# The mixers' channel-major projections and half of the gates, taken first as pairs of blocks by Strassen's seven products and passed on through DRAM

## The chip, the core and the metric

The kernel runs on one core of a Trainium2 chip. The metric is the device time of one execution in microseconds (us). Before the change the median of three runs is 2567.64 us (2566.79 to 2568.14). The engines are PE (TensorE, matmuls), DVE (VectorE), ACT (ScalarE), POOL (GpSimd) and SP (SyncE, which here only issues DMAs).

## What is computed

One layer of a streaming encoder on x of 1024 tokens by 1024 channels, float32. Cut to what matters:

```python
h = rmsnorm(x)
(hg_q, hg_f, hg_i, hg_g, ml_qk, ml_v, ml_if, ml_o,
 mb_z, mb_xbc, mb_dt, gate_pre) = split(h @ w_in)       # w_in: 1024 x 13336
o_hg = hgrn2_scan(silu(hg_q), log_f(hg_f), hg_i)         # 8 heads
y_hg = rmsnorm(o_hg) * silu(hg_g)
qk   = silu(causal_dwconv(ml_qk))                        # conv of width 4 over the tokens
y_ml = rmsnorm(mlstm_scan(qk, ml_v, ml_if)) * sigmoid(ml_o)                     # 4 heads
xbc  = silu(causal_dwconv(mb_xbc))                       # conv of width 4
y_mb = rmsnorm((ssd_scan(xbc, mb_dt) + d * xs) * silu(mb_z))                    # 4 groups
gates = sigmoid(gate_pre)                                # 3 x 1024 channels
mixed = gates[0]*(y_hg @ w_br_hg) + gates[1]*(y_ml @ w_br_ml) + gates[2]*(y_mb @ w_br_mb)
x = x + mixed @ w_out
x = x + (silu(u_g) * u_v) @ w_down                       # u = causal_dwconv(rmsnorm(x) @ w_up)
return rmsnorm(x)
```

## The kernel before

Channels lie on the 128 partitions, tokens along the free dimension. A weight block is 128x1024: all 1024 inputs (eight k tiles of 128) for 128 output channels. Every operand of a large product is split into two parts (`split`, L98 to L100): `hi` is a copy by ACT in the type fp32r, `lo` the rest, by DVE; a product is then hi·hi + hi·lo + lo·hi, three matmuls. `gemm` (L136) multiplies one block with all tokens: 8 k tiles x 3 x 2 halves of 512 tokens = 48 matmuls of 128x512 into `ps_g`, two banks of PSUM (`pg`, two such buffers). `gemm_tok` (L168) makes values with tokens on partitions, from pairs of blocks `w_v`. `weight` (L104 to L112) loads a block on SP's queue into `w_raw` (pool `wr`, three buffers) and splits it into `w_hi`, `w_lo` (pool `ws`, two).

The stages follow one another. `first` loads and normalizes x, splits it into h (four tiles of 128x8x512) and makes the first head's blocks f and q and its values. Then come 8 HGRN2 heads (`hg_head`), 4 mLSTM heads (`ml_head`) and 4 Mamba-2 groups (`mb_group`); after them the branches, each with its gate (`gate`, one block each, 24 in all), w_out, and the MLP. Each mixer makes its own blocks: an HGRN2 head three (f, q, g), an mLSTM head four (two with a conv of width 4, whose later taps are `scalar_tensor_tensor` operations at L502), a Mamba group four, all with a conv: 24 + 16 + 16 = 56 blocks. So the blocks and the `w_v` products of the next head stand in PE's queue between the small matmuls of this one, and fill the time in which a mixer's own chain runs on DVE and ACT. Of an HGRN2 head these small matmuls are the transposes of `kd` (L325), six levels with `pa` (L361, L370), the output (L380, L382), and, behind its norm, the transposes of `out_ch` (L604), which go on to DRAM as `y_dram` by a DMA on POOL's queue. Of a Mamba group they are, among others, L664, L677 and L693.

What sets the order: the mixers are written one after another, and a scheduler with its own timeline reorders the instructions of each engine by their readiness; `high_priority` lets the loading and splitting of weights come 200 places earlier. Each engine then runs its queue strictly in order. `mp` are the mixers' buffers (BUFS: one to four of a name).

## Time and profile before

| | |
|---|---|
| median of three runs | 2567.64 us |
| the profiled execution | 2567.49 us, of which the span is 2565.7 us |
| busy: PE, PE's weight loads, DVE, ACT, POOL | 2537.4, 2177.3, 1282.1, 882.1, 21.8 us |
| mean DMA rate | 64 GB/s |

The span is the profiler's stretch from the first to the last recorded work; 1.8 us lie around it. A busy time is the sum of an engine's instructions, and engines overlap. The chain that ended last is followed back from the last instruction, at each step to what released it. "Lnnn" is a line of the kernel; the lines of before and of the changed kernel are numbered apart.

### The profile page before, as it was taken

The numbers are of one execution on the slowest core, as the hardware profiler recorded it, in microseconds if no ns is written. First come the engines' busy times: TensorE is split into PE (matmuls) and PEld (weight loads), VectorE is DVE, ScalarE is ACT, GpSimd is POOL, SyncE is SP. The second block draws the span as 40 slices with busy tenths as digits, with TensorE's granted clock in tenths as the row PEclk, the third lists the DMA queues.
The fourth block names the chain that finished last, engine by engine and source line by source line (L and its number), as shares of the span: only waits on it lengthen the run. The fifth ranks groups of instructions, "written<-read, shape, count | busy, mean of one in ns | idle before, by whom it ended". The sixth has DMA issues, their size and how long they took to land.

```text
span 2565.7 us, 30851 instructions
## 1 busy us (share of the span) xinstructions
PE 2537.4 (99%) x13304; PEld 2177.3 (85%) x13304; DVE 1282.1 (50%) x1586; ACT 882.1 (34%) x1055; POOL 21.8 (1%) x35
## 2 busy tenths in 40 slices
PE   8999999999999999999999999999999999999998
PEld 7898989898889899899888888888788888888886
DVE  6676767773334466666412223235644444434446
ACT  5444444553343346445312112123332212121212
POOL 1000000000000000000000000000000000000000
PEclk8999999999999999999999999999999999999998
DMA  3011111111121122212412213132211111111111
GB/s 140 33 42 42 42 42 42 52 50 65 59 74 67 41 90 83 83 50 74 132 50 80 80 46 115 50 107 99 66 50 50 50 44 48 49 50 50 50 50 66
DMA packets 47592, 163.59 MB, mean 64 GB/s; under 512 B 5448, under 2 KB 6088, under 8 KB 47456
## 3 DMA queue, kind: packets, MB, share of 16 engines
q1 hardware_dynamic: 44000, 149.04, 17.2%
q0 software_dynamic: 3456, 12.58, 1.3%
q8 instruction: 104, 1.70, 0.3%
q14 instruction: 32, 0.26, 0.0%
HBM read 144.72 MB, written 16.88 MB: 63 GB/s over the span
## 4 chain that ended last, share of the span: by engine, by line
PE 97%; DVE 2%; ACT 1%; issue 0%; DMA 0%; DVEq 0%; SPq 0%; ACTq 0%
PE ps_g L136 70%; PE ps_g L168 9%; PE ps_m L136 5%; PE ps_m L361 3%; PE ps_m L693 1%; PE ps_m L168 1%; PE ps_m L370 1%; PE ps_m L604 1%; PE ps_m L575 1%; PE ps_m L380 1%; PE ps_m L333 0%; PE ps_m L555 0%; PE ps_m L577 0%; PE ps_m L677 0%; PE ps_m L664 0%; PE ps_m L382 0%
## 5 line engine op out<-in xcount | busy, mean ns | idle before, releaser
L136 PE MATMUL ps_g<-h,w_hi 128*128 128x512 f32 x2592 | 722.0, 396 | 3.5 <-DVE h L100 2.0
L99 ACT CAST w_hi<-w_raw 128x1024 fp32r<-128x1024 f32 x209 | 218.5, 1046 | 1049.0 <-PE ps_g L136 938.5
L136 PEld LDWEIGHTS ps_g<-h,w_hi 128*128 128x128 f32 x2592 | 484.4, 188 | 103.4 <-ACT h L99 3.1
L100 DVE TENSOR_TENSOR w_lo<-w_raw,w_hi 128x1024 fp32r<-128x1024 f32 x209 | 255.3, 1222 | 536.6 <-ACT w_hi L99 536.3
L136 PE MATMUL ps_g<-h,w_lo 128*128 128x512 f32 x1296 | 411.0, 394 | 0.0
L136 PE MATMUL ps_g<-p_hi,w_hi 128*128 128x512 f32 x1088 | 338.2, 390 | 0.7 <-DVE u L502 0.5
L136 PE MATMUL ps_g<-p_lo,w_hi 128*128 128x512 f32 x1088 | 337.6, 389 | 0.8 <-DVE p_lo L100 0.8
L136 PE MATMUL ps_g<-p_hi,w_lo 128*128 128x512 f32 x1088 | 337.8, 389 | 0.0
L136 PEld LDWEIGHTS ps_g<-h,w_lo 128*128 128x128 f32 x1296 | 243.7, 188 | 50.4
L168 PE MATMUL ps_g<-w_hi,h 128*128 128x256 f32 x1408 | 261.1, 284 | 0.0
L136 PEld LDWEIGHTS ps_g<-p_hi,w_hi 128*128 128x128 f32 x1088 | 204.1, 188 | 44.1 <-ACT w_hi L99 0.9
L136 PEld LDWEIGHTS ps_g<-p_lo,w_hi 128*128 128x128 f32 x1088 | 204.2, 188 | 43.6 <-DVE p_lo L100 1.1
L136 PEld LDWEIGHTS ps_g<-p_hi,w_lo 128*128 128x128 f32 x1088 | 204.1, 188 | 42.6 <-DVE w_lo L100 0.3
L168 PEld LDWEIGHTS ps_g<-w_hi,h 128*128 128x128 f32 x1408 | 221.3, 192 | 0.6
L168 PE MATMUL ps_g<-w_lo,h 128*128 128x256 f32 x704 | 200.1, 284 | 0.0
L168 PEld LDWEIGHTS ps_g<-w_lo,h 128*128 128x128 f32 x704 | 134.9, 192 | 0.5
L502 DVE SCALAR_TENSOR_TENSOR u<-ps_g,c_vec,u 128x1023 f32<-128x1023 f32 (+2 forms) x90 | 113.0, 1255 | 5.2 <-ACT u L498 3.7
L857 DVE TENSOR_TENSOR x<-ps_g,x 128x1024 f32<-128x1024 f32 x40 | 48.9, 1223 | 99.9 <-PE ps_g L136 99.9
L136 PE MATMUL ps_g<-a_hi,w_hi 128*128 128x512 f32 x288 | 88.8, 389 | 1.6 <-DVE x L857 1.6
L136 PE MATMUL ps_g<-a_lo,w_hi 128*128 128x512 f32 x288 | 88.7, 389 | 0.0
L136 PE MATMUL ps_g<-a_hi,w_lo 128*128 128x512 f32 x288 | 88.7, 389 | 0.0
L756 DVE TENSOR_TENSOR gate<-ps_g,gate 128x1024 f32<-128x1024 f32 x16 | 19.6, 1225 | 128.0 <-PE ps_g L136 128.0
(279 smaller groups left out, 2838.9 us busy)
## 6 DMA issues: line engine op xcount, KB each, us to landing
w_raw<-w_up SPq DMA_DIRECT2D x44, 512.0 KB, 3.4
w_raw<-w_hg SPq DMA_DIRECT2D x24, 512.0 KB, 3.4
w_raw<-w_v SPq DMA_DIRECT2D x24, 512.0 KB, 3.5
ta<-rows SPq DMA_DIRECT2D x24, 512.0 KB, 4.6
w_raw<-w_gate SPq DMA_DIRECT2D x24, 512.0 KB, 3.5
w_raw<-w_br SPq DMA_DIRECT2D x24, 512.0 KB, 3.5
w_raw<-y_dram SPq DMA_DIRECT2D x24, 512.0 KB, 3.5
w_raw<-w_down SPq DMA_DIRECT2D x22, 512.0 KB, 3.4
```

The lines of the kernel that those rows point to most:

```text
L99: self.nc.scalar.copy(out=hi, in_=src)
L100: (eng or self.nc.vector).tensor_tensor(out=lo, in0=src, in1=hi.bitcast(F32), op=ALU.subtract)
L136: self.nc.tensor.matmul(out=out, lhsT=w[:, ks], rhs=rhs(part, kt, ts), start=kt == 0 and w is hi and part == 0, stop=kt == kts - 1 and w i ...
L168: self.nc.tensor.matmul(out=out, lhsT=self.h[hf][part][:, 4 * i + k, o:o + P], rhs=w[:, ks], start=start and k == 0 and w is hi and part = ...
L361: nc.tensor.matmul(out=pa[0:m, c], lhsT=z[:, c * P:c * P + m], rhs=part(1)[:, c], start=True, stop=True)
L370: nc.tensor.matmul(out=pa[:, j], lhsT=c3(k)[:, c + j], rhs=qs[:, c + j], start=True, stop=True)
L380: nc.tensor.matmul(out=po[:, j], lhsT=A[:, c], rhs=v[:, c, vs], start=True, stop=c == 0)
L502: nc.vector.scalar_tensor_tensor(out=out[:, a:ts.stop], in0=ps[:, a - d:ts.stop - d], scalar=w(d), in1=out[:, a:ts.stop], op0=ALU.mult, op ...
L575: nc.tensor.matmul(out=po, lhsT=A[:, c], rhs=v[:, c], start=True, stop=c == 0)
L604: nc.tensor.transpose(out=pt[:, j], in_=src(4 * hf + j), identity=self.ident)
L693: nc.tensor.matmul(out=pa[:, c], lhsT=A[:, c], rhs=xd[:, c, hl * 64:hl * 64 + 64], start=True, stop=True)
L857: nc.vector.tensor_tensor(out=x2[j], in0=ps, in1=x2[j], op=ALU.add)
```

## The change

A pair of neighbouring blocks, 256 output channels, is now multiplied with all tokens by Strassen's scheme (in Winograd's form). The pair is cut in four parts by k half and block, h in four by k half and token half. Seven products of 4 k tiles x 3 matmuls of 128x512, with sums and differences of parts, replace the eight that two blocks take (96 matmuls become 84). The differences of h (t1 to t4, split into hi and lo) are made once, in `first`. For each pair, `operands` splits one block as it is (`w`), one half of the other (`q`), and makes four half-block sums on DVE, which are split as `s` and `r`; `w` has two buffers, `q`, `s` and `r` one. `pair_gemm` issues the seven products, with three half-block copies by ACT and four half-block sums by DVE between them, and a last copy by ACT.

`projections` runs between `first` and the mixers. It takes 33 pairs: 11 of HGRN2 (its first two blocks are still made in `first`), 4 of mLSTM's output gates, 6 of the branch gates (blocks 12 to 23), and 12 with a conv (4 of mLSTM, 8 of Mamba). The activations and convs are done there, and each result goes to DRAM by a DMA on POOL's queue (`keep`). The mixers fetch them on SP's queue (`fetch`). Values of the first two pairs of HGRN2 heads go through DRAM too. The other 12 gates are made by `gemm` between the HGRN2 heads (`GATES_AT`); all 24 are fetched in the branches. The mixers' buffers are allocated only after the pairs, since the t tiles (`tp`) and the pairs' buffers (`a1`) lie in their place.

Where the order moves. On PE, at the start of the projections, behind the norm of the second half of h: before, `h_84` to `h_87` are h's four tiles, and the matmuls alternate between halves.

```order
L136 MATMUL ps_g<-h_84,w_hi 128x512 x2
L136 MATMUL ps_g<-h_85,w_hi 128x512
L136 MATMUL ps_g<-h_84,w_lo 128x512
L136 MATMUL ps_g<-h_84,w_hi 128x512
L136 MATMUL ps_g<-h_85,w_hi 128x512
L136 MATMUL ps_g<-h_84,w_lo 128x512
```

After, the same place holds the value products of the second pair of HGRN2 heads, and the pairs follow; the first mixer stands behind them all:

```order
L172 MATMUL ps_g<-h,w_hi 128x512 x2
L172 MATMUL ps_g<-h,w_lo 128x512
L172 MATMUL ps_g<-h,w_hi 128x512 x2
L172 MATMUL ps_g<-h,w_lo 128x512
L172 MATMUL ps_g<-h,w_hi 128x512 x2
L172 MATMUL ps_g<-h,w_lo 128x512
```

So no block product of `gemm` is left beside the pairs. On DVE, in the middle of `projections`, where a conv pair meets the next pair's operands (`gate` is a pair's result, L161 makes the sums, L102 the lo parts, L636 is the conv's taps, `u` a partial result):

```order
L102 TENSOR_TENSOR q_lo<-w_raw,q_hi 128x512
L161 TENSOR_TENSOR w_raw<-w_raw 128x512 x2
L185 TENSOR_TENSOR gate<-ps_g,u 128x512
L636 SCALAR_TENSOR_TENSOR gate<-c,c_vec,gate 128x1023
L102 TENSOR_TENSOR s_lo<-w_raw,s_hi 128x1024
L636 SCALAR_TENSOR_TENSOR gate<-c,c_vec,gate 128x1022
L102 TENSOR_TENSOR r_lo<-w_raw,r_hi 128x1024
L636 SCALAR_TENSOR_TENSOR gate<-c,c_vec,gate 128x1021
L102 TENSOR_TENSOR w_lo<-w_raw,w_hi 128x1024
L161 TENSOR_TENSOR w_raw<-w_raw 128x512
L185 TENSOR_TENSOR u<-ps_m,u 128x512
L161 TENSOR_TENSOR w_raw<-w_raw 128x512
```

The conv's taps, which before stood beside a mixer's own work (L502), here stand between the lo parts of the next pair's s, r and w. On PE, at the end of the fourth HGRN2 head, before: the output's last matmuls, then block products, then the transposes of the norm (L604):

```order
L136 MATMUL ps_g<-h_84,w_hi 128x512
L136 MATMUL ps_g<-h_86,w_hi 128x512
L136 MATMUL ps_g<-h_85,w_hi 128x512
L136 MATMUL ps_g<-h_87,w_hi 128x512
L136 MATMUL ps_g<-h_84,w_lo 128x512
L136 MATMUL ps_g<-h_86,w_lo 128x512
L136 MATMUL ps_g<-h_84,w_hi 128x512
L136 MATMUL ps_g<-h_86,w_hi 128x512
L136 MATMUL ps_g<-h_85,w_hi 128x512
L136 MATMUL ps_g<-h_87,w_hi 128x512
L136 MATMUL ps_g<-h_84,w_lo 128x512
L604 MATMUL ps_m<-c_ident,num 128x128 x8
```

After, the last output matmuls (L514, L516), the norm's transposes (L731) and the next head's kd transposes (L459) follow directly; L235 is the value product `w_v`:

```order
L516 MATMUL ps_m<-C,qe 128x128
L514 MATMUL ps_m<-v,hgA_5196 128x128
L516 MATMUL ps_m<-C,qe 128x128
L514 MATMUL ps_m<-v,hgA_5196 128x128
L516 MATMUL ps_m<-C,qe 128x128
L514 MATMUL ps_m<-v,hgA_5196 128x128
L516 MATMUL ps_m<-C,qe 128x128
L731 MATMUL ps_m<-c_ident,num 128x128 x8
L459 MATMUL ps_m<-c_ident,ta 128x128 x7
L235 MATMUL ps_g<-w_hi,h 128x256
L235 MATMUL ps_g<-w_lo,h 128x256
L235 MATMUL ps_g<-w_hi,h 128x256 x2
```

The block products that stood ahead of the norm's transposes are gone. On PE, in the last two Mamba groups, before: block products between the groups' small matmuls (L677, L693):

```order
L136 MATMUL ps_g<-h_87,w_hi 128x512
L136 MATMUL ps_g<-h_84,w_lo 128x512
L677 MATMUL ps_m<-C,q 128x256
L136 MATMUL ps_g<-h_86,w_lo 128x512
L136 MATMUL ps_g<-h_84,w_hi 128x512
L136 MATMUL ps_g<-h_86,w_hi 128x512
L136 MATMUL ps_g<-h_85,w_hi 128x512
L136 MATMUL ps_g<-h_87,w_hi 128x512
L136 MATMUL ps_g<-h_84,w_lo 128x512
L693 MATMUL ps_m<-v,z 128x64 x16
L136 MATMUL ps_g<-h_86,w_lo 128x512
L136 MATMUL ps_g<-h_84,w_hi 128x512
```

After, the two groups' small matmuls stand alone (L755 transposes, L771 and L788 products of B, C and values, L801 and L817 the outputs, L731 the final transposes):

```order
L755 MATMUL ps_m<-c_ident,k 128x128 x8
L771 MATMUL ps_m<-q,k 128x128 x8
L788 MATMUL ps_m<-v,kT 128x256 x7
L801 MATMUL ps_m<-C,q 128x256 x7
L817 MATMUL ps_m<-v,z 128x64 x32
L731 MATMUL ps_m<-c_ident,num 128x128 x16
L755 MATMUL ps_m<-c_ident,ta 128x128 x16
L755 MATMUL ps_m<-c_ident,k 128x128 x8
L771 MATMUL ps_m<-q,k 128x128 x8
L788 MATMUL ps_m<-v,kT 128x256 x7
L801 MATMUL ps_m<-C,q 128x256 x7
L817 MATMUL ps_m<-v,z 128x64 x32
```

No block or value product stands between them there. The diff, cut to its core:

```diff
-        self.wr = ctx.enter_context(tc.tile_pool(name="wr", bufs=3))
+        self.wr = ctx.enter_context(tc.tile_pool(name="wr", bufs=4))
...
+    def operands(self, pool, srcs):
+        nc = self.nc
+        with self.tc.high_priority(offset=200):
+            raw = []
+            for src in srcs:
+                raw.append(self.wr.tile([P, 1024], F32, name="w_raw"))
+                nc.sync.dma_start(out=raw[-1], in_=src)
+            (a1, a2), (b1, b2) = [(w[:, 0:HALF], w[:, HALF:]) for w in raw]
+            new = lambda own, name, n: [own.tile([P, n], F32R, name=f"{name}_{e}", align_bytes=ALIGN)
+                                        for e in ("hi", "lo")]
+            wa = new(self.ws, "w", 1024)
+            self.split(*wa, raw[0])
+            qb = new(pool, "q", HALF)
+            self.split(*qb, b2)
+            for out, x, y, op in ((a1, a1, b1, ALU.subtract), (b1, b1, b2, ALU.add), (b2, b2, a1, ALU.subtract),
+                                  (a2, a2, b2, ALU.subtract)):
+                nc.vector.tensor_tensor(out=out, in0=x, in1=y, op=op)
+            s12, s34 = new(pool, "s", 1024), new(pool, "r", 1024)
+            self.split(*s12, raw[1])
+            self.split(*s34, raw[0])
+        return wa, s12, s34, qb
+    def product(self, w, at, b, out, start=True, stop=True):
+        for k in range(4):
+            ks = slice(at + k * P, at + k * P + P)
+            for i, (x, y) in enumerate(((0, 0), (0, 1), (1, 0))):
+                self.nc.tensor.matmul(out=out, lhsT=w[x][:, ks], rhs=b[y][:, k], start=start and k == i == 0,
+                                      stop=stop and k == 3 and i == 2, skip_group_check=True)
+    def pair_gemm(self, pool, srcs, outs):
+        nc = self.nc
+        wa, s12, s34, qb = self.operands(pool, srcs)
+        b11, b21, b22, t1, t2, t3, t4 = self.bs
+        ps = self.pg.tile([P, T], F32, name="ps_g")
+        x, y = ps[:, 0:HALF], ps[:, HALF:]
+        z, v = (self.pm.tile([P, HALF], F32, name="ps_m") for _ in range(2))
+        oa, ob = outs
+        tmp = lambda: pool.tile([P, HALF], F32, name="u", bufs=4)
+        add = lambda out, p, q: nc.vector.tensor_tensor(out=out, in0=p, in1=q, op=ALU.add)
+        u = []
+        def keep():
+            u.append(tmp())
+            nc.scalar.copy(out=u[-1], in_=x)
+        self.product(wa, 0, b11, x)
+        keep()
+        self.product(wa, HALF, b21, y)
+        add(oa[:, 0:HALF], y, u[0])
+        self.product(s12, HALF, t2, x, start=False)
+        keep()
+        self.product(s12, 0, t1, z)
+        add(u[1], z, u[1])
+        self.product(s34, 0, t3, x, start=False)
+        keep()
+        add(ob[:, HALF:], z, u[2])
+        self.product(s34, HALF, b22, v)
+        add(oa[:, HALF:], v, u[1])
+        self.product(qb, 0, t4, x, start=False)
+        nc.scalar.copy(out=ob[:, 0:HALF], in_=x)
...
+            (x11, x21), (x12, x22) = [[x[:, ks] for ks in (k1, k2)] for x in xs]
+            for i, (out, p, q) in enumerate(((x11, x12, x11), (x12, x22, x12), (x22, x22, x11), (x21, x21, x22))):
+                to = ts[(0, 2, 1, 3)[i]]
+                for k in range(0, KT // 2, 2):
+                    ks = slice(k, k + 2)
+                    nc.vector.tensor_tensor(out=out[:, ks], in0=p[:, ks], in1=q[:, ks], op=ALU.subtract)
+                    self.split(to[0][:, ks], to[1][:, ks], out[:, ks])
...
+            def evac(cs, ps):
+                g = self.gp.tile([P, T], F32, name="gate", bufs=3)
+                nc.scalar.copy(out=g, in_=ps.rearrange("p c x -> p (c x)"))
+                self.keep(self.v_d[1, cs.start // 4], g)
+            self.gemm_tok(ins["w_v"][2:4], evac)
...
+    def keep(self, dst, src):
+        self.nc.gpsimd.dma_start(out=dst, in_=src)
+    def fetch(self, dst, src):
+        self.nc.sync.dma_start(out=dst, in_=src)
...
+        for b in range(GATES, 24, 2):
+            plain.append([(ins["w_gate"][i], self.gate_d[i], AF.Sigmoid) for i in (b, b + 1)])
+        jobs, at = [], 0
+        for i, p in enumerate(plain):
+            jobs.append(p)
+            if (i + 1) * len(conv) // len(plain) > at:
+                jobs.append(conv[at])
+                at += 1
+        for job in jobs:
+            is_conv = len(job[0]) == 4
+            tile = lambda: self.gp.tile([P, T], F32, name="gate", bufs=3)
+            outs = [pool.tile([P, T], F32, name="c", bufs=2) if is_conv else tile() for _ in job]
+            self.pair_gemm(pool, [j[0] for j in job], outs)
+            for c, (_, dst, *how) in zip(outs, job):
+                if is_conv:
+                    g = tile()
+                    self.conv(g, c, *how, 4)
+                    nc.scalar.activation(out=g, in_=g, func=AF.Silu)
+                else:
+                    g = c
+                    nc.scalar.activation(out=g, in_=g, func=how[0])
+                self.keep(dst, g)
...
-        ps = begun[0] if begun else self.gemm(wb[3 * hd], self.rhs_h)
         f = mp.tile([P, T], F32, name="ta")
-        nc.scalar.activation(out=f, in_=ps, func=AF.Sigmoid)
-        ps = begun[1] if begun else self.gemm(wb[3 * hd + 1], self.rhs_h)
+        self.fetch(f, self.hg_d[3 * hd])
         qs = mp.tile([P, NC_, 192], F32, name="q")
         q = qs[:, :, 0:P]
-        nc.scalar.activation(out=q, in_=c3(ps), func=AF.Silu)
-        ps = self.gemm(wb[3 * hd + 2], self.rhs_h)
+        self.fetch(q, self.hg_d[3 * hd + 1].rearrange("p (c t) -> p c t", t=P))
         g = self.gp.tile([P, T], F32, name="gate", bufs=3)
-        nc.scalar.copy(out=g, in_=ps)
-        nc.scalar.activation(out=g, in_=g, func=AF.Silu)
+        self.fetch(g, self.hg_d[3 * hd + 2])
...
+        q, k = (mp.tile([P, T], F32, name=n) for n in "qk")
+        self.fetch(q, self.ml_d[4 * hd])
+        self.fetch(k, self.ml_d[4 * hd + 1])
...
+        def channel(j, name):
             t = mp.tile([P, T], F32, name=name)
-            self.conv(t, ps, "mb_conv", blk, 4)
-            nc.scalar.activation(out=t, in_=t, func=AF.Silu)
+            self.fetch(t, self.mb_d[4 * g + j])
...
+    def gates(self, n):
+        for _ in range(min(n, GATES - self.gates_done)):
+            i = self.gates_done
+            self.gates_done += 1
+            ps = self.gemm(self.ins["w_gate"][i], self.rhs_h)
+            g = self.gp.tile([P, T], F32, name="gate", bufs=3)
+            self.nc.scalar.activation(out=g, in_=ps, func=AF.Sigmoid)
+            self.keep(self.gate_d[i], g)
     def gate(self, i):
-        ps = self.gemm(self.ins["w_gate"][i], self.rhs_h)
         g = self.gp.tile([P, T], F32, name="gate", bufs=3)
-        self.nc.scalar.activation(out=g, in_=ps, func=AF.Sigmoid)
+        self.fetch(g, self.gate_d[i])
...
+GATES_AT = (2, 2, 2, 2, 1, 1, 1, 1)
+GATES = 12
...
+                with tc.tile_pool(name="tp", bufs=1, **right) as tp:
+                    t.first(hp, tp)
+                    with tc.tile_pool(name="a1", bufs=1, **left) as pool:
+                        t.projections(pool)
...
+                        t.hg_head(mp, hd, v)
+                        t.gates(GATES_AT[hd])
```

## Rows read from the trace of the kernel before

**Rows 1.** The page: busy time by engine, and tenths busy in 40 slices.

```profile
PE 2537.4 (99%) x13304; PEld 2177.3 (85%) x13304; DVE 1282.1 (50%) x1586; ACT 882.1 (34%) x1055; POOL 21.8 (1%) x35
...
DVE  6676767773334466666412223235644444434446
PEclk8999999999999999999999999999999999999998
```

**Rows 2.** Longest waits of PE: total us, times, longest us.

```profile
PE ps_m L192 <- DVE n_t L189: 3.3, 1, 3.3
```

**Rows 3.** The chain that ended last: start us, us, what.

```profile
588.17 21.78 PE ps_g L136 x96
644.02 11.51 PE ps_g L168 x96
1242.19 490.54 PE ps_g L136 x2164
```

**Rows 4.** Busy time of each engine in four stretches.

```profile
core 0: us, PE busy (x) PEld busy (x) DVE busy (x) ACT busy (x) POOL busy (x), PEclk, DMA share, GB/s
0.00:50.00 50.00, 40.19 (x214) 34.04 (x215) 36.84 (x59) 26.29 (x42) 6.91 (x9) 0.86 0.45 168
85.00:545.00 460.00, 458.31 (x2949) 410.65 (x2948) 329.54 (x547) 221.96 (x228) 5.82 (x9) 1.00 0.13 43
895.00:1250.00 355.00, 355.00 (x2185) 319.34 (x2183) 232.53 (x283) 183.67 (x287) 5.31 (x10) 1.00 0.25 85
1250.00:1700.00 450.00, 450.00 (x1987) 372.63 (x1986) 108.22 (x91) 78.36 (x78) 0.00 (x0) 1.00 0.21 70
```

**Rows 5.** All starts of one line: duration ns min/median/max, first to last us.

```profile
L325 PE MATMUL ps_m<-c_ident,ta x56: 270/273/273, 84.1 to 533.7; 128*128 128x128 f32 x56
...
L660 DVE TENSOR_TENSOR v<-b,mb_col x8: 1216/1223/1226, 925.2 to 1185.9; 128x1024 f32<-128x1024 f32 x8
```

**Rows 6.** Groups by form: engine, operation, out<-in xcount, busy us, mean ns.

```profile
L100 DVE TENSOR_TENSOR w_lo<-w_raw,w_hi 128x1024 fp32r<-128x1024 f32 x209 | 255.3, 1222 | 536.6 <-ACT w_hi L99 536.3
...
L99 ACT CAST w_hi<-w_raw 128x1024 fp32r<-128x1024 f32 x209 | 218.5, 1046 | 1049.0 <-PE ps_g L136 938.5 <-PE ps_g L168 44.6 <-issue 42.5
...
L136 PE MATMUL ps_m<-p_hi,w_lo 128*128 128x512 f32 x128 | 49.8, 390 | 0.0
...
L502 DVE SCALAR_TENSOR_TENSOR q<-ps_g,c_vec,q 128x1022 f32<-128x1022 f32 x8 | 10.2, 1279 | 0.2
...
L99 ACT CAST h<-n_t 128x512 fp32r<-128x512 f32 x16 | 9.8, 619 | 13.2 <-DVE n_t L225 12.8
...
L189 DVE TENSOR_TENSOR n_t<-n_t 128x512 f32<-128x512 f32 x14 | 9.7, 690 | 6.0 <-ACT n_t L188 5.1
...
L100 DVE TENSOR_TENSOR h<-n_t,h 128x512 fp32r<-128x512 f32 x12 | 8.8, 774 | 0.0
```

**Rows 7.** Timeline, end of the first HGRN2 head: start us, us, what.

```profile
124.64 0.39 PE L382 MATMUL ps_m<-C,qe 128*128 128x128 f32 x2
...
136.38 1.22 DVE L386 TENSOR_TENSOR num<-num,r 128x1024 f32<-128x1024 f32 x1
137.51 1.22 DVE L318 TENSOR_TENSOR ta<-ta,k 128x1024 f32<-128x1024 f32 x1
```

**Rows 8.** Waits of DVE in the Mamba groups.

```profile
DVE v L660 <- ACT b L632: 27.3, 4, 6.8
DVE C L666 <- PE ps_m L664: 12.1, 4, 3.0
```

**Rows 9.** SP's queue waits, and DMA issues with KB and us to landing.

```profile
SPq L108 <- DVE w_lo L100: 2050.7, 190, 29.0
...
y_dram<-gate POOLq DMA_DIRECT2D x16, 512.0 KB, 3.0
```

More of the change, by code (lines that the diff above doesn't have):

```diff
@@ L238, in first @@
             begun = [(w, self.rhs_h, self.gemm_w(w, self.rhs_h, spans=HALVES[:1])) for w in ws]
[L239 to L240 removed]
+            flat = [t.rearrange("p k t -> p (k t)") for t in ts[3]]
+            vw = [self.weight_(ins["w_v"][i], [f[:, i * 1024:(i + 1) * 1024] for f in flat]) for i in range(2)]
             dg = self.norm_sums(tmp, lambda kt: xs[1][:, kt])
@@ L278, in hg_v @@
         v = mp.tile([P, NC_, 256], F32, name="v")
+        if pair < 2:
+            for i in range(2):
+                self.fetch(v[:, 4 * i:4 * i + 4], self.v_d[pair, i].rearrange("p (c x) -> p c x", x=256))
+            return v
         def evac(cs, ps):
```

82 lines of the change are left out of this document (46 added, 36 removed).

## The prediction

> **What bounds the kernel now.** I read the page's busy times and slices first. PE is busy for 2537.4 us of a span of 2565.7 us, DVE for half of it, ACT for a third; the granted clock stands at full in every slice but the first and the last [rows 1]. The waits of PE come next: the longest is 3.3 us [rows 2], so nothing makes PE wait for long. The chain that ended last then runs nearly all on PE, through stretches of block products: 96 matmuls of L136 took 21.78 us, 2164 took 490.54 us [rows 3], both 0.2267 us each, so a block of 48 costs 10.9 us. The windows by stage say what the average hides. In the HGRN2 heads PE is busy 458 of 460 us, but DVE 330; in the Mamba groups PE 355 of 355, DVE 233; in the branches behind them DVE 108 of 450 [rows 4]. The mixers' chains on DVE and ACT are long, and they cost nothing because block products stand in PE's queue beside them. The kernel is bound by the number of matmuls, and the mixers would bound it where their filling is gone.
>
> The sum is made against the profiled execution: 2567.5 us, that is the span of 2565.7 and 1.8 around it, and within 0.1 of the median of 2567.64. A measurement of this kernel can tell about 0.2%, some 5 us, from no change.
>
> **Removed: matmuls.** 33 pairs took 96 matmuls each and take 84: 33 x 12 = 396 fewer at 0.2267 us, -89.8 us. The kind is the same (128x512 in fp32r, clock at full). Half of the products end in a one-bank `ps_m` tile; where L136 writes such a tile its matmul has 390 ns in the grouped rows [rows 6], like those into `ps_g`, so I price nothing for that. The casts and lo parts of the weights don't shrink.
>
> **Added beside the pairs: operands.** A pair holds PE for 84 x 0.2267 = 19.0 us. On DVE a plain pair has three lo parts of 1.22, one half of 0.77 and eight half-block sums of 0.69 (the nearest row is L189's): 10.0 us; a conv pair has six taps of 1.28 more, 17.6 us [rows 6]. DVE's total therefore fits under PE. What is tight is order. `q`, `s` and `r` have one buffer, and the next pair's `q` is cut ahead of its `s`. So once the last product has released `q` there run in a row: cast 0.62, lo 0.77, sum 0.69, cast 1.05, lo 1.22 = 4.35 us [rows 6]. Meanwhile PE has the next pair's first two products, which need only `w`: 24 x 0.2267 = 5.4 us. Plain pairs are in time by 1.1 us. In the 12 conv pairs a tap of 1.28 stands in the middle of that row on DVE, and ACT has the conv's passes: one tap more makes 5.6, a tap and a pass of 1.05 makes 6.7. I take 0.7 us for each, 8 us. The bounds are 0 (the scheduler's gaps fit) and 33 x 2.5 = 83 (two taps and a pass late in every pair: 4.35 + 2.56 + 1.05 - 5.4). I choose near the low end, since only conv pairs have the taps.
>
> **Added: transfers.** 84 results of 512 KB are stored and fetched. A store as this one, `y_dram` on POOL's queue, lands in 3.0 us [rows 9]. A pair of 19 us moves 2 weights in and 2 results out, 2.1 MB, 110 GB/s; the first 50 us show 168 [rows 4], so bandwidth hides it. The fetches stand on SP's queue behind weight loads that wait for a free `w_raw`, up to 29 us [rows 9]; while PE works through block products that is harmless, at the first head and the branches' start it isn't. I take 10 us for the first pair, the first head's fetches and the branches' start together, bounds 0 and 25.
>
> **Moved: the filling of the HGRN2 heads.** A head's period is 64.2 us before (eight heads' transposes from 84.1 to 533.7, over seven) [rows 5]. Less three blocks of 10.9 and half a value product of 11.5 [rows 3], its own matmuls are 20 us. Afterwards the order gives the eight heads 578 block matmuls (12 gates and the scalars) and 849 value matmuls of 0.12 us (11.51 over 96 [rows 3]): 131 + 102 = 233 us, 29 a head, so 49 us of PE. DVE had 329.5 over the 7.17 heads of its window, 46 a head [rows 4]; three lo parts go, some come: 44. PE would still be longer, if the filling stood where it is needed. It doesn't. At the end of the first head before, the last output matmul ends at 125.0, the norm's scaling on DVE at 137.6 and the next head's kd at 138.7 [rows 7]: PE can do nothing of either head for 12.6 and 13.7 us. The new order has, between the last output matmul and the norm's transposes, filling of 5.8, 0.7, 14.0, 0, 13.8, 11.5 and 0 us in heads one to seven. Less 1.6 us for transposes, holes of 6.3, 11.4, 0, 12.1, 0, 0.6 and 12.1 are left: 43 us. Bounds: 30 and 60; DVE's queue is lighter there than before by the weights' lo parts, on the other hand the chain of Ln, scan and Exp cannot be shortened. Within the levels I take 5 us (0 to 15), as each level passes DVE and ACT and 29 us of filling are spread over it. The eighth head has nothing but 81 value matmuls, 9.7 us, in its tail: 20 + 9.7 against DVE's 44 leaves up to 14, some 20 with a full tail; some of DVE's work runs ahead under the seventh head. I take 12, bounds 5 and 20.
>
> **Moved: the filling of the Mamba groups.** Four groups share the window of 355 us [rows 4]; their period is 87 [rows 5]. Less 16 blocks of 10.9 and eight halves of value products of 11.5, the groups' own matmuls are (355 - 174 - 92) / 4 = 22 us. On DVE a group has 232.5 / 4 = 58.1; without 12 taps (15.3) and four lo parts (4.9) [rows 6], 37.9 are left. By the order the last two groups have no filling at all, so they take their chain's time: 2 x 37.9 and half of the waits that DVE shows there already, (27.3 + 12.1) / 4 = 9.9 a group [rows 8], is 86 us against 44 of PE. The start of the first of them still lies beside the filling of the group before, 4 us; 38 are left, bounds 25 and 50. The first two groups and the mLSTM heads keep value products, and I price nothing there.
>
> **The sum.** 2567.5 - 89.8 + 8 + 43 + 5 + 12 + 38 + 10 = 2594 us.
>
> **Rivals.**
> Rival A: the chains shrink with the load. The tail of 13.7 us was read where DVE also had the weights' lo parts in its queue, at 1.22 each, and where nothing hurried it. With the lighter queue the tails leave half (22), the levels 0, the eighth head 5, the groups 25, the pairs 0, the rest 3: 55 us, 2533 (2520 to 2562). For it: DVE is busy only 72% of the HGRN2 stage [rows 4]. Against it: the tail's operations depend on each other across DVE and ACT, and the scheduler put the filling elsewhere. It decides as soon as all holes together are under 90 us.
>
> Rival B: the granted clock falls in the pauses. In the first 50 us, where PE is first idle and then interrupted, the clock was 0.86 on average [rows 4], which is 7 us lost in a stretch of 50. The rest of before has no such pause, so no row shows the price inside a kernel. With eight places (five tails, the eighth head, two groups) that is 56 us, half of it under waits that exist anyway: 28 more, 2622; all of it 2650. The Trainium skill ("TensorE: Matmul & The Clock Gate", section "Why this matters for your kernels") says that idle gaps between bursts of matmuls throw the engine back to the lower rate; before, with no pause over 3.3 us inside, cannot show whether it holds here, and only the start agrees with it (0.86).
>
> Rival C: every pair is late. If the one-buffered operands are late by 2.5 us in all pairs, 83 stand in place of 8: 2669. For it: one row of five dependent operations against a cover only 1.1 us longer. Against it: plain pairs have nothing in between.
>
> **How the numbers follow.** Forecast 0.48, A 0.25, B 0.15, C 0.12. The predicted time is the forecast's, 2594; its own range is 2560 to 2635. The range of 2525 to 2660 takes in nearly all of A and B, and leaves out half of C and the far ends. Faster by over 0.2%: A but for its upper edge, and a little of the forecast's lower end, 0.26. Within 0.2% (2562 to 2573): the forecast's lower end, 0.09. Slower: the rest, 0.65.
>
> **What the new profile would show.** PE's count is 396 block matmuls lower and its busy time some 2450 us. In the stretch of the pairs PE waits little: under 10 us in all, most for `s`; Rival C shows 2 us or more for `s` or `r` at each pair. In the HGRN2 stage PE has waits of around 10 us for `num` and `ta` at the ends of the second, fourth and seventh head, and none at the third and fifth; under Rival A these are under 6. In the last two groups PE is under 60% busy over some 85 us. Rival B shows a clock under full in the slices with holes. I am wrong if the holes together are under 90 us, or if the largest stand beside the pairs.

## The result, and the profile after

The changed kernel takes 2702.48 us (median of 4 runs, 2698.44 to 2706.7), before 2567.89: a ratio of 1.0525 (1.0507 to 1.0543), slower by 134.6 us. The direction was forecast, the size was not: 2594 was predicted, with a range up to 2660.

First the page of the changed kernel: busy time by engine, then the tenths of busy time in 40 slices and the granted clock of TensorE. It answers to [rows 1].

```profile
PE 2518.1 (93%) x12908; PEld 2140.6 (79%) x12908; DVE 1535.8 (57%) x1932; ACT 997.2 (37%) x1245; POOL 73.4 (3%) x119
...
PE   8999999999998798878979769999999999999998
...
DVE  7455665666567677785566672354554443434435
...
PEclk8999999999999898988989779999999999999998
```

PE's busy time fell by only 19 us, though 90 us of matmuls are gone, and the span is 182 us longer than it. PE pauses in slices 13 to 24, and in slices 14 to 24 the granted clock is mostly under full. Next, what PE waited for (total us, times, longest us); [rows 2] had nothing over 3.3:

```profile
PE ps_m L731 <- DVE num L520: 28.0, 5, 10.4
PE ps_g L172 <- ACT u L190: 22.4, 33, 0.8
PE ps_m L459 <- DVE ta L452: 21.1, 5, 7.7
PE ps_m L788 <- DVE C L795: 15.5, 4, 7.7
PE ps_m L731 <- DVE num L720: 13.7, 2, 10.7
PE ps_m L731 <- DVE num L840: 10.9, 1, 10.9
```

The first and third row are the ends of HGRN2 heads (the norm's transposes, the next head's kd), the second stands in the pairs, once in each, the fourth and sixth in Mamba groups, the fifth in mLSTM heads. None of them is DMA.

To see which stretch lost what, I cut both traces at two places: the first kd transposes of the first head (end of the pairs), and the first block product of the branches. PE's work in a stretch is each matmul at the pitch that it has at full clock in the trace of before (0.2267 us for 512 columns, 0.120 for 256 in fp32r, 0.111 for 128 columns in float32, 0.112 for 64, and so on); what is left of the stretch is lost. The third stretch ends with the last matmul, some 9 us before the end of the span.

| stretch | before, us | after, us | PE's work before, after | lost before, after |
|---|---|---|---|---|
| start, and the pairs | 84.1 | 791.5 | 65.8, 736.2 | 18, 55 |
| mixers | 1158.8 | 804.1 | 1150.5, 617.0 | 8, 187 |
| branches to the end | 1313.5 | 1095.3 | 1300.3, 1073.5 | 13, 22 |

The work fell by 89.9 us in all, as forecast (89.8). The losses grew by 37, 179 and 9 us, 224 in all, where 116 were forecast. The mixers hold most of it. Here are their three parts (HGRN2, mLSTM, Mamba) in windows, of before:

```profile
core 0: us, PE busy (x) PEld busy (x) DVE busy (x) ACT busy (x) POOL busy (x), PEclk, DMA share, GB/s
84.00:587.00 503.00, 501.31 (x3285) 452.50 (x3284) 357.53 (x591) 243.43 (x254) 5.82 (x9) 1.00 0.13 44
587.00:910.00 323.00, 323.00 (x1789) 283.17 (x1788) 135.38 (x157) 111.75 (x145) 4.78 (x9) 1.00 0.20 67
910.00:1243.00 333.00, 333.00 (x2078) 300.83 (x2077) 221.57 (x273) 171.29 (x275) 3.19 (x6) 1.00 0.23 76
```

and of the changed kernel (same columns):

```profile
791.00:1255.00 464.00, 394.93 (x2716) 365.84 (x2715) 337.95 (x579) 195.27 (x208) 10.94 (x19) 0.90 0.21 75
1255.00:1400.00 145.00, 129.57 (x924) 123.18 (x922) 81.56 (x112) 49.90 (x89) 3.72 (x7) 0.95 0.37 135
1400.00:1595.00 195.00, 153.38 (x1051) 142.34 (x1051) 135.03 (x202) 97.66 (x206) 4.25 (x8) 0.84 0.30 103
```

Before, PE is busy in all of each part, and its work sets the length. After, an mLSTM part of 323 us has become 145 and a Mamba part of 333 has become 195, but the HGRN2 part went from 503 only to 464, with PE's work in it down from 496 to 357 us. Of the 106 us lost there PE stands idle for 69 (464.00 less 394.93); the other 37 are matmuls that took longer than their pitch at full clock.

### The profile page after: what moved, and what is told of

Its sections match the earlier page's. It is cut to its first block, busy times and chain, and to the rows that moved or that the text cites. A ratio compares the mean times of both kernels' runs of the same rounds, so it can differ in the third digit from the quotient of the medians.

```text
span 2699.8 us, 31302 instructions
## 1 busy us (share of the span) xinstructions
PE 2518.1 (93%) x12908; PEld 2140.6 (79%) x12908; DVE 1535.8 (57%) x1932; ACT 997.2 (37%) x1245; POOL 73.4 (3%) x119
## 4 chain that ended last, share of the span: by engine, by line
PE 70%; issue 23%; DVE 4%; ACT 2%; DMA 1%; POOL 1%; SPq 0%; DVEq 0%; POOLq 0%; ACTq 0%
PE ps_g L138 36%; PE ps_g L172 17%; PE ps_m L172 6%; PE ps_m L138 5%; PE ps_g L235 3%; PE ps_m L235 1%; PE ps_m L495 1%; ACT u L190 1%; PE ps_m L504 0%; POOL y_dram L739 0%; DMA y_dram<-ta 0%; DMA w_raw<-w_hg 0%; PE ps_m L273 0%; DVE z L92 0%; DMA w_raw<-y_dram 0%
## 5 line engine op out<-in xcount | busy, mean ns | idle before, releaser
L101 ACT CAST w_hi<-w_raw 128x1024 fp32r<-128x1024 f32 x174 | 182.2, 1048 | 787.9 <-PE ps_g L138 525.0
L102 DVE TENSOR_TENSOR w_lo<-w_raw,w_hi 128x1024 fp32r<-128x1024 f32 x174 | 212.6, 1222 | 389.9 <-ACT w_hi L101 385.8
L235 PE MATMUL ps_g<-w_hi,h 128*128 128x256 f32 x1408 | 274.2, 292 | 12.7 <-ACT gate L776 5.7
L235 PEld LDWEIGHTS ps_g<-w_hi,h 128*128 128x128 f32 x1408 | 226.9, 195 | 15.9 <-ACT gate L776 6.1
L235 PE MATMUL ps_g<-w_lo,h 128*128 128x256 f32 x704 | 205.2, 291 | 1.0 <-DVE w_lo L102 1.0
L172 PE MATMUL ps_g<-h,w_hi 128*128 128x512 f32 x528 | 162.6, 389 | 0.0
L138 PE MATMUL ps_g<-h,w_hi 128*128 128x512 f32 x480 | 137.3, 398 | 6.9 <-DVE h L102 3.9
L235 PEld LDWEIGHTS ps_g<-w_lo,h 128*128 128x128 f32 x704 | 137.5, 195 | 2.1 <-DVE w_lo L102 1.4
L636 DVE SCALAR_TENSOR_TENSOR u<-ps_g,c_vec,u 128x1023 f32<-128x1023 f32 (+2 forms) x90 | 113.0, 1255 | 5.2 <-ACT u L632 3.7
L172 PEld LDWEIGHTS ps_g<-h,w_hi 128*128 128x128 f32 x528 | 99.1, 188 | 20.5
L138 PEld LDWEIGHTS ps_g<-h,w_hi 128*128 128x128 f32 x480 | 90.1, 190 | 28.4 <-DVE h L102 4.7
L636 DVE SCALAR_TENSOR_TENSOR gate<-c,c_vec,gate 128x1023 f32<-128x1023 f32 (+2 forms) x72 | 92.2, 1280 | 24.0 <-ACT gate L632 23.6
L172 PE MATMUL ps_g<-t,q_hi 128*128 128x512 f32 x264 | 85.2, 404 | 21.7 <-ACT u L190 21.7
L172 PE MATMUL ps_g<-h,w_lo 128*128 128x512 f32 x264 | 102.7, 389 | 0.0
L161 DVE TENSOR_TENSOR w_raw<-w_raw 128x512 f32<-128x512 f32 x132 | 91.4, 692 | 6.6 <-DMA w_raw<-w_ml 1.8
```

Source lines behind the costliest of these rows:

```text
L101: self.nc.scalar.copy(out=hi, in_=src)
L102: (eng or self.nc.vector).tensor_tensor(out=lo, in0=src, in1=hi.bitcast(F32), op=ALU.subtract)
L138: self.nc.tensor.matmul(out=out, lhsT=w[:, ks], rhs=rhs(part, kt, ts), start=kt == 0 and w is hi and part == 0, stop=kt == kts - 1 and w i ...
L161: nc.vector.tensor_tensor(out=out, in0=x, in1=y, op=op)
L172: self.nc.tensor.matmul(out=out, lhsT=w[x][:, ks], rhs=b[y][:, k], start=start and k == i == 0, stop=stop and k == 3 and i == 2, skip_grou ...
L235: self.nc.tensor.matmul(out=out, lhsT=self.h[hf][part][:, 4 * i + k, o:o + P], rhs=w[:, ks], start=start and k == 0 and w is hi and part = ...
```

## The experiments

All are changes of the changed kernel. A stretch is named as in the table. The diffs show what differs from it.

**e1: plain blocks in the place of the pairs.**

```diff
-            self.pair_gemm(pool, [j[0] for j in job], outs)
-            for c, (_, dst, *how) in zip(outs, job):
+            for c, (w, dst, *how) in zip(outs, job):
+                nc.scalar.copy(out=c, in_=self.gemm(w, self.rhs_h))
```

> The changed kernel, but each pair is two plain block products of 48 matmuls in the same place (with the same casts, convs, activations, stores and fetches), and the differences of h are not made. The theory is that the pairs themselves save most of what they should and lose about 1.06 us each (35 us in 33 pairs) in a stall before the seventh product, and that all the rest of the loss lies in the mixers, which are the same here: 396 matmuls x 0.2267 = +89.8, less 35 = +55, so about 2757 us (2740 to 2770), with the mixers' stretch of some 840 us as in the changed kernel. The rival, that the seven products with their sums cost as much as they save (late operands, fuller DVE, one-bank tiles), gives 2702 or less.

Measured: 2747.44 us, 45 more than the changed kernel. The mixers' stretch is the same, 806.1 us. The stretch of the blocks lost 20 us in place of 55, so some 36 us are the pairs' own loss; 10 us of the missing difference are gate matmuls that now stand in the mixers' stretch (628 us of work in place of 617), where they add almost nothing. So the pairs do save time, about half of what their count says, and what makes the kernel slower lies elsewhere.

**e2: PE in the written order inside a pair.**

```diff
-        self.product(wa, 0, b11, x)
+        with self.tc.manual_schedule(engines={mybir.EngineType.PE}):
+            self.product(wa, 0, b11, x)
...
```

> The changed kernel with PE kept to the written order inside a pair, so that the product of r and h into its own bank stands between the fifth product and the seventh, which both accumulate in the same half of ps_g, with a copy by ACT between them. Theory: the stall of 1.06 us in each pair is the copy's time in which the seventh product can't start; with 12 other matmuls (2.7 us) in between it goes, 33 x 1.06 = 35 us: 2667 us (2662 to 2675). Rival (the one of the prediction): the operands are late, so the stall comes back as a wait for s at the third product, since q is released at the same time relative to the pair: 2690 to 2703.

The stall that this edit removes, in the timeline of the changed kernel (start us, us, engine, what; the idle time before it and who ended it in brackets):

```profile
133.83 0.39 PE L172 MATMUL ps_g<-t,r_lo 128*128 128x512 f32 x1
134.26 1.07 ACT L190 COPY u<-ps_g 128x512 f32<-128x512 f32 x2 [0.93 <-PE ps_g L172]
134.89 0.73 PE L172 MATMUL ps_g<-t,q_hi 128*128 128x512 f32 x2 [0.68 <-ACT u L190]
```

The fifth product's last matmul (into `ps_g`) starts at 133.83, ACT copies that half to `u` from 134.26, and the seventh product, which accumulates in the same half, starts at 134.89, 1.06 us after the one before it instead of 0.23. The scheduler had put the sixth product, which goes to another bank, ahead of the fifth. Measured: 2710.59 us, above both ranges and nearest to the rival's. Both were right in mechanism. Most plain pairs now take 19.04 to 19.4 us in place of 20.01, and 19.04 is exactly 84 x 0.2267; but a conv pair takes 21.2 to 22.9 in place of 20.5, for the reason that the prediction gave. PE's waits:

```profile
PE ps_g L172 <- DVE s_lo L102: 20.8, 11, 1.9
```

In 11 of the conv pairs PE now waits up to 1.9 us for the lo part of s, which stands behind a tap on DVE. One stall had covered the other: from the first pair to the last the time is 673.7 us, against 674.2 in the changed kernel. What is slower stands behind them, where the edit changes nothing but what the scheduler makes of it: 6 us more between the last pair and the first kd transposes, and 813.2 us for the mixers in place of 804.1.

**e5: as e2, with two buffers for q.**

```diff
-            qb = new(pool, "q", HALF)
+            qb = new(pool, "q", HALF, 2)
...
-        tmp = lambda: pool.tile([P, HALF], F32, name="u", bufs=4)
+        tmp = lambda: pool.tile([P, HALF], F32, name="u", bufs=2)
```

> As e2 (PE in the written order inside a pair), with two buffers for q, and two instead of four for the partial results u, which makes room for it. In e2 a plain pair took 19.04 us, exactly its 84 matmuls, and each of the 12 conv pairs some 2.8 us more, waiting for the lo part of s. Theory: that wait is the row that starts when the last product releases q (cast, lo, sum, cast, lo) with the conv's taps in it on DVE; with a second q the row starts earlier and the wait goes: 12 x 2.8 = 34 us less than e2, 2677 us (2670 to 2685). Rival: DVE and ACT simply have too much in a conv pair, or s itself is the buffer that binds: 2700 to 2711.

Measured: 2680.05 us, as expected. Every pair now takes 19.04 us, conv or not, and in the window of the pairs PE is busy throughout (columns as in the windows above):

```profile
96.00:740.00 644.00, 643.16 (x2837) 532.23 (x2837) 396.81 (x464) 324.60 (x379) 35.52 (x66) 1.00 0.32 108
```

So the two limits were the copy between the fifth and seventh product, and the row that starts when q is released. With both gone the pairs give all that their count promises: from the first to the last they take 639 us in place of 674, 35 less. The kernel gains only 22, as 10 us more pass between the last pair and the first kd transposes and 5 more in the mixers. It is still 4.4% slower than before (1.0438, 1.0424 to 1.0452), by 112 us, and that lies in the mixers (809 us for 615 us of work). Edits to the pairs alone moved the mixers' stretch to 806, 813 and 809 us (e1, e2, e5), so a difference of under 10 us there says nothing.

**e3: all 24 gates beside the mixers.**

```diff
-GATES_AT = (2, 2, 2, 2, 1, 1, 1, 1)
-GATES = 12
+GATES_AT = (2, 2, 2, 2, 2, 2, 1, 1)
+ML_AT = (1, 1, 2, 1)
+MB_AT = (2, 2, 1, 0)
+GATES = 24
...
                         t.ml_head(mp, hd)
+                        t.gates(ML_AT[hd])
...
                         t.mb_group(mp, g)
+                        t.gates(MB_AT[g])
```

> The changed kernel with all 24 gates made by plain block products beside the mixers (two or one behind each HGRN2 head, each mLSTM head and the first three Mamba groups), none as a pair. Work: 12 more blocks of 10.9 (131 us), 6 pairs of 20.0 fewer (120 us): +11. Theory: the loss in the mixers is missing filling, 126 us of idle PE and some 60 us of matmuls at a lower granted clock between 775 and 1620 us; 131 us more of filling, put into the tails that had none, remove 60 to 80% of the 187: 2583 us (2550 to 2620), and the granted clock is 0.98 or more in the mixers. Rival: the mixers wait for their fetches through DRAM or for DVE's chain wherever PE stands, so the filling only adds: 2680 to 2715.

Measured: 2624.09 us. The mixers' stretch became 43 us longer, 847, with 130 us more work in it, while the pairs' stretch became 120 shorter: two thirds of the added filling cost nothing. That is less than the theory's 2583, and the waits say why:

```profile
PE ps_m L731 <- DVE num L520: 28.0, 4, 12.9
PE ps_m L459 <- DVE ta L452: 8.8, 4, 3.3
```

The tails of some heads still pause (in the second head the scheduler moved the gates to other places), the longest for 12.9 us. More filling helps where it stands, not by its sum.

**e4 and e6: matmuls of constants in the pauses.** They separate the pause from the lower clock that goes with it.

```diff
+    def dummies(self, out, n):
+        for _ in range(n):
+            self.nc.tensor.matmul(out=out, lhsT=self.ones, rhs=self.ones, start=True, stop=True)
...
+            if hf == 0 and (br, blk) in BARE:
+                self.dummies(pt[:, 0], 92 if br else 64)   # e6: 46 if br else 26
...
+BARE = {(0, 1), (0, 3), (0, 6), (1, 4), (2, 4)}
```

The same call stands ahead of the next head's kd transposes, with 48 (e6: 28).

> The changed kernel with matmuls of constants, whose result is overwritten, in five tails without filling: ahead of the norm's transposes (64 of 128x128 at 0.11 us in the second, fourth and seventh HGRN2 head, 92 in the third mLSTM head and the third Mamba group) and 48 ahead of the next head's kd transposes. They do no useful work and stand where PE waits. Theory: the lower granted clock after a pause is a cost of its own, some 60 us in the mixers; where PE doesn't pause the clock stays full, so the time falls by 35 us (15 to 55) though PE does more: 2667 us, and PE's clock in the HGRN2 stretch rises from 0.90-0.94 to 0.98 or more. Rival: the clock costs nothing, since DVE's chain sets the time there anyway: 2700 to 2710.

Measured: 2748.19 us, which neither theory gave. The row of the added line (duration min/median/max in ns, first and last start):

```profile
L728 PE MATMUL ps_m<-ones x1040: 272/275/528, 892.7 to 1605.1; 128*128 128x128 f32 x174
```

520 matmuls left 1040 records, each at a pitch of 0.111 us: one costs 0.22 us, so I had added 115 us to pauses of 61. e6 mends the size.

> As e4, with fewer matmuls of constants. In e4 one of them cost 0.22 us, twice what was assumed (two records each), so 520 of them took 115 us where the pauses were 61 us. Now 26 and 28 in the three HGRN2 heads and 46 in the mLSTM head and the Mamba group: 254, 56 us, about the length of the pauses. Theory that the clock after a pause has a price of its own: the pauses are filled and nothing else changes, so what is gained is the clock's: 2670 us (2655 to 2685). Rival, for which e4 speaks (its mixers grew by 45 us, only 10 less than the 54 by which its constants exceeded the pauses): most of the slow matmuls stand where DVE's chain sets the time, and the gain is 10 us or less: 2690 to 2705.

Measured: 2704.98 us, the same as without them. The three parts of the mixers, to be compared with those of the changed kernel above:

```profile
791.00:1255.00 464.00, 423.11 (x3033) 396.30 (x3032) 337.73 (x579) 197.25 (x209) 10.94 (x19) 0.94 0.22 76
1255.00:1400.00 145.00, 139.53 (x1025) 133.48 (x1024) 80.60 (x110) 49.27 (x87) 3.72 (x7) 0.99 0.39 135
1400.00:1595.00 195.00, 165.35 (x1134) 153.96 (x1132) 133.50 (x198) 97.89 (x208) 4.25 (x8) 0.86 0.30 103
```

The granted clock rises from 0.90 to 0.94 and from 0.95 to 0.99, and PE is busy for 28 and 10 us more. The windows are cut at the same times, so the lengths have to be read at the work itself: from the first kd transposes to mLSTM's first transposes 463.3 us pass in both kernels, from there to Mamba's first transposes 145.2 without the constants and 144.8 with them, from there to the first branch product 195.6 and 197.3. (Head by head, the three with constants took 3.8 to 4.1 us longer and those behind them 1.3 to 7.6 less, as the kd transposes move with the constants ahead of them.) The rival holds: the slower matmuls stand where PE would wait anyway. My theory that the clock has a price of its own falls, as far as the clock rose; in the Mamba part it went only from 0.84 to 0.86, and what full clock would give there isn't shown.

**e7: mLSTM heads and Mamba groups make their own blocks again.** `ml_head` and `mb_group` as before the change; 17 pairs are left.

```diff
-        self.fetch(q, self.ml_d[4 * hd])
...
+            ps = self.gemm(wb[4 * hd + j], self.rhs_h)
+            t = mp.tile([P, T], F32, name="qk"[j])
+            self.conv(t, ps, "ml_conv", 4 * j + hd, 4)
...
```

> The changed kernel, but the mLSTM heads and Mamba groups make their own 32 blocks as before the change; 17 pairs are left (HGRN2 and 12 of the gates), the order of PE inside them as in the changed kernel. Work: 16 pairs of 84 matmuls become 32 blocks of 48, +43.5 us; the stalls of 16 pairs go, 4 x 1.0 and 12 x 1.4 = -21. Theory: of the 200 us that PE loses in the mixers' stretch some 90 stand in the mLSTM heads and Mamba groups and come from the missing blocks; 80 of them go: 2702 + 43 - 21 - 80 = 2644 us (2630 to 2665), while the tails of the second, fourth and seventh HGRN2 head keep their 10 to 14 us. Rival: the loss there is the fetches' and the chain's, 20 us or less go: 2705 us or more.

Measured: 2657.98 us. The mixers lose 118 us in place of 187; the gain there is 69 of the 80 expected. What is left stands in the HGRN2 heads: their waits are much like those of the changed kernel,

```profile
PE ps_m L729 <- DVE num L511: 22.3, 4, 10.8
PE ps_m L450 <- DVE ta L443: 13.1, 3, 7.7
```

with the same longest pauses of about 11 and 8 us.

**e9: two of the six levels of an HGRN2 head left out.**

```diff
         for li, h in enumerate(HG_LEVELS):
+            if h in (8, 4):
+                continue
```

> The changed kernel with two of the six levels of each HGRN2 head left out (8 and 4; that part of the computation is missing from the output). A level is four half-length operations of DVE of 0.69 us and one of 0.86, a pass of ACT of 1.05, and 16 matmuls of 0.11 us. Left out: 16 levels, 58 us of DVE, 17 of ACT, 28 of PE. Theory after e6: the heads take the time of their own chain over DVE and ACT (55 to 60 us a head, whether PE has 40 or 52 us of work in it), so the time falls by DVE's part or more: 2645 us (2625 to 2655). Rival: what sets the heads' time is PE with its pauses at the heads' ends (tails and the wait for the fetch), which stay as they are: 2675 us or more.

Measured: 2628.91 us, 73.6 less. The kd transposes (first to last start, us), of the changed kernel and of e9, give the heads' period:

```profile
L459 PE MATMUL ps_m<-c_ident,ta x56: 270/374/448, 791.5 to 1209.5; 128*128 128x128 f32 x56
```

```profile
L459 PE MATMUL ps_m<-c_ident,ta x56: 271/273/448, 792.7 to 1144.6; 128*128 128x128 f32 x56
```

(1209.5 - 791.5) / 7 = 59.7 us a head, against (1144.6 - 792.7) / 7 = 50.3. Two levels are worth 9.4 us a head on average. (The mean contains the sixth period, 79.7 us, in which the operations of `scalars` stand on DVE; the others are 47.2 to 60.2.) Their operations in the changed kernel (busy us, mean ns):

```profile
L489 ACT ACTIVATE z<-z 128x1024 f32<-128x1024 f32 x48 | 49.7, 1054 | 63.2 <-DVE z L488 62.8
...
L490 DVE TENSOR_TENSOR z<-z,k 128x512 f32<-128x512 f32 x48 | 33.0, 687 | 12.7 <-ACT z L489 12.5
...
L548 DVE COPY_PREDICATED hgA<-c_hmask,ps_m 128x512 f32<-128x512 uint8 x32 | 27.4, 857 | 41.5 <-PE ps_m L495 41.3
```

Four half-length operations of DVE, one predicated copy and one Exp of ACT: 4 x 0.686 + 0.857 + 1.054 = 4.65 us a level, 9.3 for two. That this sum meets the 9.4 is in part chance: the seven periods fell by 5.5 to 16.6 us each, and the same rows show that DVE waited only 12.5 us in all for the 48 passes of Exp, which took 49.7, but 41.3 us for the level's matmuls (L495). The seven periods of the changed kernel and of e9 in windows (columns as above):

```profile
791.00:1208.00 417.00, 355.52 (x2462) 327.73 (x2460) 309.70 (x529) 182.91 (x188) 10.94 (x19) 0.91 0.22 77
```

```profile
792.00:1143.00 351.00, 318.18 (x2239) 292.04 (x2237) 264.56 (x456) 163.31 (x170) 10.41 (x18) 0.97 0.26 89
```

Of the 66 us that went, 45 are busy time of DVE, and 21 are time in which DVE waited (107 in the changed kernel, 86 in e9). So a head takes the time of a chain, of which DVE's operations are the largest part and in which DVE also waits for ACT and for PE's small matmuls, which stand in PE's queue among the filling. The amount of PE's work doesn't set it: that fell by only 2 x 1.8 us a head. How the waits divide between ACT and PE isn't shown.

**e10: the fetches on POOL's queue.**

```diff
     def fetch(self, dst, src):
-        self.nc.sync.dma_start(out=dst, in_=src)
+        self.nc.gpsimd.dma_start(out=dst, in_=src)
```

> The changed kernel with the fetches of the stored results on POOL's queue in place of SP's, where they stand behind loads of weights that wait for a free buffer. Rival of the chain theory: the mixers and the branches wait for late fetches, so the time falls by 20 us or more. Theory: DVE waits only some 14 us in all for a fetch in the mixers, and those are for a free buffer, not for the queue; the time stays, 2695 to 2710 us.

Measured: 2708.77 us: no gain. So it isn't SP's queue with its weight loads that makes the fetches late, and DVE's waits for them in the mixers of the changed kernel are short:

```profile
DVE ta L437 <- DMA ta<-hg_dram: 6.8, 3, 2.4
DVE ta L662 <- DMA ta<-rows: 3.9, 1, 3.9
DVE ta L809 <- DMA ta<-rows: 3.6, 3, 2.3
```

But e10 leaves in place what the fetch of the next head's f waits for. In the changed kernel it stands in the queue behind the fetch of q for the head after that one, and this waits for a buffer until the present head's last matmuls of q (L504) are through:

```profile
887.36 0.81 PE L504 MATMUL ps_m<-q,k 128*128 128x192 f32 x4
888.20 0.53 SPq L352 DMA_DIRECT2D q<-hg_dram  x1
888.79 0.65 SPq L352 DMA_DIRECT2D ta<-hg_dram  x1
893.33 0.81 DVE L437 TENSOR_SCALAR ta<-ta,hg_olb,hg_sm 128x1024 f32<-128x1024 f32 x1 [2.24 <-DMA ta<-hg_dram]
```

In e10 the same two start at 889.5 and 890.4 us, on POOL's queue. What an earlier fetch of f would give wasn't tried.

**e8: a version that keeps the filling.** 15 pairs, none with a conv, in written order; `ml_head` keeps its two conv blocks and `mb_group` all four as before the change; three gates behind each HGRN2 head.

```diff
-            conv.append([(ins["w_ml"][b + j], self.ml_d[b + j], "ml_conv", 4 * j + hd) for j in range(2)])
...
-        for g in range(4):
-            b = 4 * g
-            for js in ((2, 3), (0, 1)):
...
-GATES_AT = (2, 2, 2, 2, 1, 1, 1, 1)
-GATES = 12
+GATES_AT = (3, 3, 3, 3, 3, 3, 3, 3)
+GATES = 24
```

> A version meant to keep the filling: only 15 pairs without a conv (11 of HGRN2, 4 of mLSTM's output gates), PE in written order inside them, so 19.04 us each; the mLSTM heads and Mamba groups make their other blocks themselves as before the change; all 24 gates are made beside the HGRN2 heads, three behind each, in the place of the three blocks that each head made itself, and fetched in the branches. Theory: 15 x 12 x 0.2267 = 41 us of matmuls saved against the kernel before, filling as before in every mixer except for places where the order of readiness leaves a tail short, 20 to 30 us: 2553 us (2535 to 2575), that is faster than before by 0.5%. Rival: the tails of the heads pause as in e3 whatever stands behind a head (loss in the mixers' stretch 90 us more than before): 2615.

Measured: 2555.22 us (2554.04 to 2555.73), a ratio of 0.995 (0.9937 to 0.9962) to before: faster than both kernels, than the one before by only 0.5%, and within 3 us of the expectation. PE and its clock in the 40 slices, and the mixers' window:

```profile
PE   8999999999999999999999899999999999999998
...
PEclk8999999999999999999999899999999999999999
```

```profile
415.00:1450.00 1035.00, 1025.95 (x6426) 923.16 (x6424) 684.34 (x998) 488.53 (x632) 25.30 (x46) 0.99 0.25 84
```

PE is busy for 1026 of 1035 us there. Seven heads have periods of 60 to 74 us with 53 to 71 us of PE's work in them.

**e11: further in the same direction.** Eight more pairs (with a conv: mLSTM's q and k, Mamba's B and C), gates spread 3 and 2 over the HGRN2 heads and one behind each mLSTM head, two buffers for q.

> As e8, going further: 23 pairs (11 of HGRN2, 8 of mLSTM, 4 of Mamba's B and C blocks), the two buffers for q of e5, since 8 of them have a conv, and the gates spread over the heads: 3 and 2 in turn beside the HGRN2 heads, one beside each mLSTM head. Theory: 8 more pairs save 8 x 2.72 = 22 us of matmuls against e8, and the mixers' stretch, which has some 1000 us of PE's work in e8 against some 800 of the chains, keeps enough to hide them; some 10 us are lost to new pauses: 2543 us (2533 to 2556). Rival: the filling is again short in the mLSTM heads and last Mamba groups and 30 us or more come back: 2560 or more.

Measured: 2621.89 us; the rival's side, and far above the 2560 from which it began.

```profile
PE ps_g L236 <- DVE ta L637: 23.7, 3, 7.9
PE ps_m L732 <- DVE num L721: 13.0, 1, 13.0
```

The first row is new: in the Mamba groups value products wait behind the taps of the two blocks that the groups still make. The mixers hold 833 us of PE's work and take 939. Whether another place of the gates would mend it wasn't tried.

## Why the prediction was wrong

**Right.** 396 matmuls went, at 0.2267 us. The tails of the HGRN2 heads paused where the order had said, in the first, second, fourth and seventh head and not in the third and fifth: 47 us in the eight pauses over 2 us, against 43 forecast. The last two Mamba groups, with no filling, took 79 us against 86 forecast. For transfers 10 us were put; 8 are lost at the start of the branches, and DVE waits 14 us for fetches in the mixers, of which part may count. DVE's chain was seen as the next bound. Rival A fell: the tails didn't shrink to half with DVE's lighter queue.

**Wrong, the main step: how much PE loses in the mixers (98 forecast, 179 measured).** Three terms of it were mis-sized.

- *HGRN2: 43 + 5 + 12 = 60 forecast, 99 measured* (106 lost after, 7 before). The prediction's own figures gave the part a length of 8 x 49 + 60 = 452 us, near the 464 that it has, but by luck: PE's work in it was put at 49 us a head, and it is 45 (357 / 8), and the loss is larger by nearly as much. 479 block matmuls fall in that part, not 578 (the other 99 stand between the last pair and the first kd transposes), and a head's own matmuls are 18.4 us, not the 20 that were left of the period. The tails' 43 held (47), the last head's 12 came out as 19; the term that failed is the 5 us for everything else in the heads, where some 33 were lost. I found the pauses at the tails and put 5 us on everything else, since the head's filling (29 us) seemed enough; yet filling that isn't at hand in each of the six levels leaves PE idle there, or slow beside a chain that has the time. e9 shows that a head takes its chain's time, over DVE, ACT and its own matmuls. Of the first five periods, those with 40 us of PE's work took 55.5 and 56.7 us, those with 51 to 52 took 57.5 to 60.2. The sixth took 79.7, as it did before (80.8), when PE was full in it: `scalars` stands there, DVE is busy for 65 us in place of 39 to 44, and PE now loses 16 of the 106 us. The prediction spread that work over the heads. The shortest head of before, 55.3 us from its kd transposes to the next, with PE full, had already given an upper bound for that chain; I didn't read it from the rows.
- *mLSTM: nothing forecast, 18 measured*, in the third head above all, whose tail has no filling: a pause of 10.7 us.
- *Mamba: 38 forecast, 62 measured.* The last two groups lost 40 of it, near the term; the first two, which I priced at nothing because they keep value products, 22. e7 shows that in mLSTM and Mamba the missing blocks did it: 69 us come back with them.

**Wrong by a mechanism that I didn't see: the pairs (8 forecast, 36 measured by e1).** The forecast's row for q and s exists, and costs 11 of the 12 conv pairs 2.2 to 3.8 us each once it is exposed (e2). In the changed kernel another wait stood ahead of it, in every pair: the seventh product accumulates in the bank that ACT has yet to copy, and starts 1.06 us after the matmul ahead of it in place of 0.23. Rival C had the right count of pairs for the wrong reason. The order had shown that the sixth product stands ahead of the fifth; I counted matmuls there and not who reads the bank between them.

**Rival B.** The clock did fall, to 0.84 in the Mamba part, where PE pauses most. In e6 it rose in the HGRN2 and mLSTM parts and their lengths stayed (463.3 and 463.3 us, 145.2 and 144.8), so there it cost nothing that can be told from no change; in the Mamba part it stayed low. The Trainium skill ("TensorE: Matmul & The Clock Gate", section "Why this matters for your kernels") says that idle gaps between bursts of matmuls return the engine to its lower rate; the trace agrees with the rule (0.84 to 0.95 in the three parts with pauses, 1.00 in the same parts before). As a price in the first two it would have been counted twice, since PE waits there in any case.

**What is settled and what isn't.** That the amount of PE's work doesn't set the HGRN2 heads' time, and their chain does, is shown (e6, e9); which of the waits in that chain could be shortened is not. For mLSTM and Mamba e7 shows that the missing blocks made the loss; that the chain sets the time there is argued from it. Not tried were another order of DVE and ACT, the levels' matmuls ahead of the filling in PE's queue, and an earlier fetch of f.

## What to carry to other kernels

Work that is taken out of a stretch in which it hid a chain saves nothing there: first find each stage's length without it (the shortest period that the trace has is an upper bound; the operations of one unit along its chain, on whichever engine, are an estimate), and take the larger of that and PE's work, stage by stage, before the saving is summed. Then move only what the stage has in excess: e8 took 15 of the 33 pairs, put the gates in the place of the blocks, and turned +5.2% into -0.5%. And where several products accumulate in one bank with copies between them, look in the order for what stands between a copy and the next product into it.

## What the runs showed of the hardware

A lower granted clock of TensorE was free where PE waited for a chain in any case: e6 raised it from 0.90 to 0.94 in a part of 463.3 us without changing its length. A float32 matmul of 128x128 constants left two records and cost 0.22 us, twice the pitch of one record (e4). Removing one of two stalls in a pair gave nothing (e2: 673.7 us for the pairs in place of 674.2), removing both gave 35 us there (e5: 639.2), since each covered the other.
